# Experts ranked by their rows, in places of 192 down to 32 rows, with four products side by side at 32 rows

## The chip, the core and the metric

The kernel runs on one core of a Trainium2 chip. The metric is the time of one execution on the device, in microseconds, as a median of three runs. TensorE multiplies matrices: the weights of a product (at most 128 rows of contraction by 128 columns) are loaded first, and the other operand of up to 512 columns streams past them into a PSUM bank. VectorE, ScalarE and GpSimd work on elements, and DMA queues bring the weights from HBM; the queue of SyncE issues the loads that matter here.

## The reference

Two transformer blocks on 512 tokens of width 1024 in float32. The first has two feed-forward layers and two attentions, the second a convolution and a chunked recurrence and then a mixture of 32 experts in four groups. Every token chooses a group, and two experts in it; each expert is a gated feed-forward layer of width 512. The change concerns only this last part.

```python
def hierarchical_moe(h, rg_w, rg_b, re_w, re_b, w_gate, w_up, w_down):
    ...
    expert_id = grp[:, None] * EXPERTS_PER_GROUP + top_idx.astype(jnp.int32)
    ...
    counts = jnp.zeros((N_EXPERTS,), jnp.int32).at[e_flat].add(1)
    starts = jnp.cumsum(counts) - counts
    ...
    def expert_block(args):
        xb, e = args
        a = xb @ w_gate[e]
        u = xb @ w_up[e]
        return (jax.nn.silu(a) * u) @ w_down[e]

    ys = lax.map(expert_block, (xs, block_expert)).reshape(n_slots, D)
    ys = ys * slot_gate[:, None].astype(ys.dtype)
    out = jnp.zeros((T, D), ys.dtype).at[slot_tok].add(ys)
...
def second_block(x, ...):
    for l in range(DEPTH):
        h = rmsnorm(x, norm_mix_g[l])
        x = x + hybrid_mixer(h, ...)
        h = rmsnorm(x, norm_ffn_g[l])
        x = x + hierarchical_moe(h, ...)
    return rmsnorm(x, final_norm_g)
```

`top_idx` are the two best experts of the chosen group, so there are 1024 pairs of token and expert. With the reference's inputs they are spread very unevenly: an expert gets between 0 and 150 rows, and five more than 64 beside the first two.

## The kernel before

`route` computes the logits, chooses, and sorts the 1024 pairs by expert: `xs` holds the chosen rows, already transposed, in the order of the experts. Since the counts are known only on the chip, the program is a fixed list of 32 steps (`SLOTS`), each with one place: a number of rows for one expert. Which expert a place gets is worked out in `route`, in a row of small VectorE operations (`wl_...`), and ends in the list `wl` (the expert and the first row of every place), which SyncE reads for the address of a load and ScalarE for the rows.

Steps 0 and 1 take up to 64 rows each of experts 0 and 1, so that their weights can be loaded before the routing is known. Of the other 30 places, five have 128 rows (steps 6, 11, 16, 21, 26) and 25 have 64. An expert with 128 rows or more takes places of 128, the rest goes to places of 64, and what doesn't fit goes through a loop behind the steps; with these inputs the loop does not run.

A place needs six tiles of 1 MB of its expert: `gate` and `up`, two each, and two of `down`. `e_advance` issues a load as soon as a buffer of the three rings (13 tiles in all) is free; a tile is given back by the product that used it last. So there are 192 loads, in the order of the steps.

Step `i` is written out in this order: gate and up of step i+1 (`e_gu`, eight chunks of 128 contraction rows), its activation (`e_act`), down of step i (`e_down`, four chunks), and `keep`. Products are in float32. At 64 rows the bank is split: gate goes to partitions 0 to 63 and up to 64 to 127, which uses two different halves of the array's columns; at 128 rows each product uses all columns and a bank of its own. Between the chunks of gate and up stand, at chunk 0, the transposes of step i's activation (`e_turn`), and behind chunks 3, 5 and 7 three of the four spreads of the place kept in the step before; the fourth stands behind the first chunk of down.

`keep` takes the result of down out of its bank in two parts, a rounded one (ScalarE, `y`) and what is left (VectorE, `y`), and builds `pick`, a matrix that says which row belongs to which token. `spread` multiplies the two, 128 tokens at a time, and VectorE adds the two banks of that to the tokens (`x`). Its products take operands of a rounded format and 128 columns of weights, and their banks come from `po` and `mm` in turn, and `tp`. There are three `mm` banks, two `sc`, two `tp` and one `po`. All products are recorded on line 302, so the tiles' names tell them apart.

## Time and profile before

| | |
|---|---|
| three runs | 2005.28, 2005.52, 2007.22 us |
| median | 2005.52 us |
| the profiled execution | 2004.82 us, its span 2003.0 us |
| busy in the span: TensorE, VectorE, ScalarE | 1894.3 (95%), 1087.9 (54%), 636.4 us (32%) |
| mean granted clock of TensorE | 0.978 |
| loads of experts | 192, of 1024 KB |

The profile is of one execution, and its times are counted from the start of its span. The experts' loads are issued from 1399.9 to 1942.8, and the products with expert weights end near 1976. The page divides the span into 40 slices: in those of the experts the loads move 355 to 420 GB/s, where the rest of the program has mostly 60 to 130.

### The profile page before, as it was taken

How to read it: one execution, taken by the hardware profiler on the slowest of the kernel's cores; microseconds unless marked ns; L12 is line 12 of the kernel's file. 1: busy time of each engine (PE TensorE's matmuls, PEld its weight loads, DVE VectorE, ACT ScalarE, POOL GpSimd, SP SyncE). 2: the span in 40 equal slices, each digit the busy share in tenths (PEclk: the TensorE clock that was granted, in tenths of full speed). 3: DMA queues.
4: the chain of work that ended last, by engine and by line, in shares of the span. 5: the costliest groups of instructions: out<-in, count | busy, mean ns of one | idle time of the engine just before them, and what ended most of it. 6: DMA issues, size and time to landing. Idle time of an engine off the chain costs nothing.

```text
span 2003.0 us, 22137 instructions
## 1 busy us (share of the span) xinstructions
PE 1894.3 (95%) x8372; PEld 1299.0 (65%) x8372; DVE 1087.9 (54%) x1655; ACT 636.4 (32%) x1006; POOL 381.8 (19%) x293
## 2 busy tenths in 40 slices
PE   7999999999999999999999988779799999999995
PEld 5888888887777788888888766657543333333331
DVE  6443344423668565443444599988544444444445
ACT  4322233325555443331223333433232111111112
POOL 2000000106654351000001456643210000000001
PEclk9999999999999999999999998889999999999997
DMA  5234222322222122222222211111799999999991
GB/s 178 85 129 153 92 97 93 126 85 93 81 68 75 64 93 97 101 89 106 86 104 101 97 63 43 42 42 54 288 355 420 419 397 391 380 397 378 384 359 43
DMA packets 52440, 337.85 MB, mean 169 GB/s; under 512 B 5868, under 2 KB 8724, under 8 KB 13804
## 3 DMA queue, kind: packets, MB, share of 16 engines
q1 hardware_dynamic: 48396, 324.04, 42.2%
q0 software_dynamic: 3072, 9.24, 1.5%
q10 hardware_dynamic: 864, 3.15, 0.4%
q8 instruction: 67, 1.10, 0.2%
q14 instruction: 41, 0.34, 0.0%
HBM read 332.18 MB, written 8.16 MB: 170 GB/s over the span
## 4 chain that ended last, share of the span: by engine, by line
PE 81%; DVE 14%; issue 2%; ACT 1%; DMA 1%; POOL 1%; SPq 0%; POOLq 0%; ACTq 0%; DVEq 0%
PE mm L302 65%; PE sc L302 8%; PE tp L302 4%; DVE conv L302 4%; PE po L302 3%; DVE qk L302 2%; DVE score L302 1%; DVE x L302 1%; DVE att_s L302 1%; DVE rs_t L302 1%; DVE rs_y L302 0%; DMA x<-in_xT_dram 0%; DVE hm L302 0%; DMA raw<-in_wd_dram 0%; DVE rs_r L302 0%
## 5 line engine op out<-in xcount | busy, mean ns | idle before, releaser
L302 PE MATMUL mm<-nhi,whi 128*128 128x512 f32 x1120 | 446.8, 399 | 13.3 <-ACT whi L356 9.4
L302 PE MATMUL mm<-nlo,whi 128*128 128x512 f32 x1120 | 439.1, 392 | 1.6 <-DVE nlo L302 1.6
L302 PE MATMUL mm<-nhi,wlo 128*128 128x512 f32 x1120 | 438.5, 392 | 0.7 <-DVE wlo L302 0.7
L356 ACT ACTIVATE whi<-raw 128x1024 fp32r<-128x1024 f32 x220 | 231.2, 1053 | 306.8 <-PE mm L302 119.0
L302 DVE TENSOR_TENSOR wlo<-raw,whi 128x1024 fp32r<-128x1024 f32 x155 | 198.1, 1279 | 208.9 <-ACT whi L356 208.9
L302 PE MATMUL mm<-eraw,xb 128*64 128x512 f32 (+1 forms) x992 | 272.9, 602 | 0.0
L302 PEld LDWEIGHTS mm<-nhi,whi 128*128 128x128 f32 x1120 | 211.8, 189 | 62.7 <-ACT whi L356 9.4
L302 PEld LDWEIGHTS mm<-nlo,whi 128*128 128x128 f32 x1120 | 211.6, 189 | 47.1 <-DVE nlo L302 4.5
L302 PEld LDWEIGHTS mm<-nhi,wlo 128*128 128x128 f32 x1120 | 211.4, 189 | 46.5 <-DVE wlo L302 1.7
L302 POOL TENSOR_TENSOR wlo<-raw,whi 128x1024 fp32r<-128x1024 f32 x65 | 163.5, 2520 | 150.9 <-ACT whi L356 125.1
L302 PEld LDWEIGHTS mm<-eraw,xb 128*64 128x64 f32 (+1 forms) x992 | 81.9, 145 | 130.3 <-issue 120.5
L302 PE MATMUL sc<-eraw,hT 128*64 128x512 f32 (+1 forms) x512 | 140.1, 602 | 0.0
L302 PE MATMUL mm<-hhi,whi 128*128 128x512 f32 x352 | 136.9, 389 | 0.0
L302 PE MATMUL mm<-hlo,whi 128*128 128x512 f32 x352 | 136.9, 389 | 0.0
L302 PE MATMUL mm<-hhi,wlo 128*128 128x512 f32 x352 | 136.9, 389 | 0.0
L302 POOL TENSOR_TENSOR acc<-sq,sq 128x512 f32<-128x512 f32 x6 | 8.7, 1456 | 579.6 <-ACT sq L455 579.6
L302 DVE TENSOR_TENSOR x<-x,po 128x512 f32<-128x512 f32 x62 | 42.6, 687 | 125.4 <-PE po L302 125.3
L302 POOL TENSOR_SCALAR rs_v<-fss 128x1 f32<-128x1 f32 x3 | 0.6, 191 | 515.0 <-ACT eraw L1882 514.8
L1699 ACT ACTIVATE xb<-xs 128x512 f32 (+1 forms) x31 | 21.9, 706 | 233.1 <-PE mm L302 233.0
L302 DVE TENSOR_TENSOR up<-mm,row 128x512 f32<-128x512 f32 x44 | 30.4, 691 | 110.8 <-PE mm L302 110.8
L302 DVE SCALAR_TENSOR_TENSOR conv<-ca,vecs,conv 128x502 f32<-128x502 f32 (+18 forms) x78 | 88.0, 1183 | 0.2
L302 DVE TENSOR_TENSOR y<-sc,y 64x512 fp32r<-64x512 f32 (+1 forms) x64 | 44.1, 689 | 80.7 <-ACT y L1774 62.3
(448 smaller groups left out, 2641.7 us busy)
## 6 DMA issues: line engine op xcount, KB each, us to landing
eraw<-in_we_dram SPq DMA_DIRECT2D x192, 1024.0 KB, 8.0
raw<-in_wd_dram SPq DMA_DIRECT2D x109, 1024.0 KB, 4.8
bias_rows<-bias_by_distance SPq DMA_DIRECT2D x4, 960.0 KB
bias<-bias_rows POOLq DMA_DIRECT2D x12, 256.0 KB, 3.1
x_rows<-x ACTq DMA_DIRECT2D x4, 512.0 KB, 3.5
x<-in_xT_dram SPq DMA_DIRECT2D x3, 512.0 KB, 8.3
raw<-in_wd_dram SPq DMA_DIRECT2D x2, 512.0 KB, 8.9
out_dram<-eraw SPq DMA_DIRECT2D x2, 512.0 KB
```

Source lines behind the costliest of these rows:

```text
L302: return f(*a, **k)
L356: self.nc.scalar.activation(hi, raw, AF.Copy)
L1699: self.nc.scalar.activation(x[:, :, 0:m], self.xs[:, :, ds(row, m)], AF.Copy)
```

## The change

Experts are ranked on the chip by the rows that are left when experts 0 and 1 have had their first 64. The expert of each rank gets a fixed set of places (`RANKS`): 128 and 64 rows for the first, 128 and 32 for the second, 128 for the third, 64 and 32 for the next five, 64 for six, and 32 for the last sixteen. With the two known ahead these are 32 steps again and 39 places: 14 of 64 rows, 22 of 32 and 3 of 128. `EXEC` gives the order of the ranks. All places of a rank stand in one step and use the same six tiles; their chunks follow each other inside the step, chunk by chunk. What is over a rank's capacity goes to the loop behind, which is rewritten for it.

At 32 rows a product has 32 columns of weights and 256 streaming columns, and four of them share a bank: gate left, gate right, up left, up right, each in 32 columns of the array (`gu_chunk`); in down, four quarters (`down_chunk`). `keep` copies and subtracts four quarters of 256 columns, and the spread of such a place uses 64 contraction rows.

The list of places is worked out with two products with triangles and ones (for what goes to the loop) and two that bring expert, first row and last row to the places, where before it was a chain of VectorE operations alone. Three compare tiles stand for two (64, 32 and 128 rows). The rows' tiles `xb` have a ring for each size.

The core of the diff (left out: the constants' new columns, other small operations of the routing, the loop, and lines that only pass the new arguments on):

```diff
-FIRST = 2
-WIDE = 5
-PLACES = 42
-SLOTS = 32
-ITEMS = FIRST + 2 * NE
-WIDE_AT = (6, 11, 16, 21, 26)
+FIRST, FIRST_ROWS = 2, 64
+RANKS = [(128, 64), (128, 32), (128,)] + [(64, 32)] * 5 + [(64,)] * 6 + [(32,)] * 16
+EXEC = (8, 14, 3, 15, 16, 0, 17, 18, 4, 19, 9, 20, 2, 21, 22, 5, 10, 23, 1, 24, 25, 6, 11, 26, 7, 27, 12, 28, 13, 29)
+NL = 32
+
+
+def place_table():
+
+    t = [(-1 - e, 0, FIRST_ROWS, 0) for e in range(FIRST)]
+    for r, ms in enumerate(RANKS):
+        for k, m in enumerate(ms):
+            t.append((r, sum(ms[:k]), m, sum(ms) if k == 0 else 0))
+    t.sort(key=lambda a: {64: 0, 32: 1, 128: 2}[a[2]])
+    of = {}
+    for w, a in enumerate(t):
+        of.setdefault(a[0], []).append((a[1], w, a[2]))
+    of = {r: [(w, m) for _, w, m in sorted(a)] for r, a in of.items()}
+    n = [sum(a[2] == m for a in t) for m in (64, 32, 128)]
+    return t, of, ((0, n[0]), (n[0], n[0] + n[1]), (n[0] + n[1], sum(n)))
+
+
+TABLE, PLACES_OF, GROUPS = place_table()
+P_L = len(TABLE)
+PLACES = P_L + NL
 RINGS = {"raw2": 9, "raw": RAW, "raw3": 2}
...
-        V.tensor_copy(cnt, c[:, 4])
-        F, W, E = FIRST, WIDE, ends
...
+        V.scalar_tensor_tensor(key, left, 32.0, down, op0=ALU.mult, op1=ALU.add)
+        V.scalar_tensor_tensor(cmp[e32, 0:32], key[e32], 1.0, idn, op0=ALU.mult, op1=ALU.mult, accum_out=kcol)
+        V.scalar_tensor_tensor(cmp[e32, 0:32], key[e32], kcol, one, op0=ALU.is_gt, op1=ALU.mult, accum_out=rank)
...
+        pt = self.tp()
+        nc.tensor.matmul(pt[0:32, 0:1], self.tri_b[e32, 0:32], ov[e32, 0:1], start=True, stop=True)
+        nc.tensor.matmul(pt[0:32, 1:2], self.ones_b[e32, 0:32], ov[e32, 0:1], start=True, stop=True)
+        V.tensor_copy(col[e32, 5:7], pt[0:32, 0:2])
...
+        nc.tensor.matmul(pt[0:PLACES, 0:3], M[e32], A[e32], start=True, stop=False)
+        nc.tensor.matmul(pt[0:PLACES, 0:3], ML[e32], B[e32], start=False, stop=True)
...
+            for a in (iota64, iota32, iota[:, 0:128]):
...
-        rest = iter(range(FIRST + WIDE, SLOTS))
-        wide = iter(range(FIRST, FIRST + WIDE))
-        self.ex = [i if i < FIRST else next(wide if i in WIDE_AT else rest) for i in range(SLOTS)]
+        self.steps = [PLACES_OF[-1 - e] for e in range(FIRST)] + [PLACES_OF[r] for r in EXEC]
+        n = len(self.steps)
         o = [(0, j) for j in range(4)]
...
+    def gu_chunk(self, m, ps, x, c, gate, up):
+        s = (c % 4) * 512
+        k = {"start": c == 0, "stop": c == KC - 1}
+        for j, w in enumerate((gate, up)):
+            if m == 32:
+                for f in range(2):
+                    a = 64 * j + 32 * f
+                    self.nc.tensor.matmul(ps[0][a:a + 32, 0:256], x[:, c, 0:32], w[:, s + 256 * f:s + 256 * f + 256], **k)
+            else:
+                o = ps[j] if m == 128 else ps[0][64 * j:64 * j + 64]
+                self.nc.tensor.matmul(o, x[:, c, 0:m], w[:, s:s + 512], **k)
+
+    def down_chunk(self, m, ps, h, c, w):
+        s = (c % 2) * 1024
+        k = {"start": c == 0, "stop": c == 3}
+        if m == 32:
+            o = (c % 2) * 64 + (c // 2) * 32
+            for g in range(4):
+                self.nc.tensor.matmul(ps[0][32 * g:32 * g + 32, 0:256], h[:, o:o + 32],
+                                      w[:, s + 256 * g:s + 256 * g + 256], **k)
+        else:
+            for f in range(2):
+                o = ps[f] if m == 128 else ps[0][64 * f:64 * f + 64]
+                self.nc.tensor.matmul(o, h[:, c * m:(c + 1) * m], w[:, s + 512 * f:s + 512 * f + 512], **k)
...
+        subs = [(m, (self.mm(), self.mm()) if m == 128 else (self.mm(),)) for _, m in self.steps[i]]
         for c in range(KC):
...
+            for (m, ps), x in zip(subs, xs):
+                self.gu_chunk(m, ps, x, c, P[i, j], P[i, j + 1])
...
+        banks = iter((self.sc, self.sc, self.po))
+        subs = [(m, tuple(next(banks)() for _ in range(2 if m == 128 else 1))) for m in ms]
...
+        y = self.yt(F32R)
+        n = 512 if m == 64 else 256
+        for g in range(128 // m):
+            a, o = slice(m * g, m * g + m), slice(m * (g ^ 1), m * (g ^ 1) + m)
+            c = slice(512 * g, 512 * g + 512) if m == 64 else slice(256 * (g % 2), 256 * (g % 2) + 256)
+            nc.scalar.activation(y[a, c], ps[0][a, 0:n], AF.Copy)
+            nc.vector.tensor_sub(y[o, c], ps[0][a, 0:n], y[a, c].bitcast(F32))
         for f in range(2):
-            y = parts[f:f + 1] if len(parts) == 2 else parts
-            r = [y[0][:, 0:512], y[0][:, 512:1024]] if len(parts) == 2 else [y[0][:, 512 * f:512 * f + 512]]
-            for i, a in enumerate(r):
-                self.nc.tensor.matmul(banks[f], w, a, start=first and i == 0, stop=last and i == len(r) - 1)
+            if m == 64:
+                parts.append([(s, y[:, 512 * f:512 * f + 512])])
+            else:
+                a = slice(64 * f, 64 * f + 64)
+                parts.append([(s[a], y[a, 0:512])])
...
+    def spread_to(self, kept, t, banks):
+
+        for f in range(2):
+            r = [a for parts in kept for a in parts[f]]
+            for i, (s, y) in enumerate(r):
+                self.nc.tensor.matmul(banks[f], s[:, t * 128:(t + 1) * 128], y, start=i == 0, stop=i == len(r) - 1)
...
-        banks = self.mm() if t % 2 else self.po(), self.tp()
+    def spread(self, kept, t, mm):
+        banks = self.mm() if mm else self.po(), self.tp()
...
+            both = i + 1 < n and sum(2 if m == 128 else 1 for _, m in self.steps[i + 1]) == 3
+            todo = []
+            if kept:
+                todo = [lambda t=t, k=kept: self.spread(k, t, t == 3 or (t == 1 and not both)) for t in range(4)]
...
+                subs = self.e_gu(i + 1, x, hook)
                 x, xn = xn, rows(i + 3)
-                hn = self.e_act(ps, fac(i + 1))
+                hn = act(i + 1, subs)
...
+            subs = self.e_down(i, hT, lambda c: c % 2 == 0 and todo and todo.pop(0)())
...
+            kept = [self.keep(m, ps, self.tok[:, w:w + 1]) for (w, _), (m, ps) in zip(self.steps[i], subs)]
```

The order of the instructions shows what this does in three places. On TensorE, in a step of 64 rows, before: `mm` from `eraw` is a chunk of gate and up, `sc` one of down, and a product from `y` and `pick` is half a spread.

```order
L302 MATMUL mm_10799<-eraw_10641,xb_10664 64x512
L302 MATMUL mm_10799<-eraw_10651,xb_10664 64x512
L302 MATMUL po_10843<-y_10794,pick_10792 128x512
L302 MATMUL tp_10844<-y_10794,pick_10792 128x512
L302 MATMUL sc_10864<-eraw_10653,hT_10803 64x512 x2
L302 MATMUL mm_10867<-y_10794,pick_10792 128x512
L302 MATMUL tp_10868<-y_10794,pick_10792 128x512
```

After, in a step of 64 and 32 rows, at a spread of a place of 64 rows (`mm_10937` is the place of 64 rows, `mm_10938` that of 32):

```order
L332 MATMUL mm_10937<-eraw_10701,xb_10763 64x512
L332 MATMUL mm_10937<-eraw_10746,xb_10763 64x512
L332 MATMUL mm_10938<-eraw_10701,xb_10774 32x256 x2
L332 MATMUL mm_10938<-eraw_10746,xb_10774 32x256 x2
L332 MATMUL po_10972<-y_10932,pick_10930 128x512
L332 MATMUL tp_10973<-y_10932,pick_10930 128x512
L332 MATMUL mm_10937<-eraw_10791,xb_10763 64x512
L332 MATMUL mm_10937<-eraw_10797,xb_10763 64x512
L332 MATMUL mm_10938<-eraw_10791,xb_10774 32x256 x2
```

Each chunk has its two products at 64 columns and then four at 32, and the spread stands between chunks as before. In the step behind it, a step of 32 rows alone, the spread of a place of 32 rows comes behind four such short chunks:

```order
L332 MATMUL mm_11084<-eraw_10812,xb_10896 32x256 x2
L332 MATMUL mm_11084<-eraw_10845,xb_10896 32x256 x2
L332 MATMUL po_11117<-y_11075,pick_11073 128x512
L332 MATMUL tp_11118<-y_11075,pick_11073 128x512
L332 MATMUL mm_11084<-eraw_10847,xb_10896 32x256 x2
L332 MATMUL mm_11084<-eraw_10877,xb_10896 32x256 x2
```

On ScalarE, `keep` before, at the end of a step of 64 rows (`sc` is the bank of down; what is waited for stands in brackets):

```order
L1774 ACTIVATE y_10694<-sc_10670 64x512 [waits PE_49]
L1774 ACTIVATE y_10694<-sc_10670 64x512 [waits DVE_49]
```

After, at the end of a step of 64 and 32 rows, from the activation of that step (`eg`) to the transposes of the next (`hT`):

```order
L1783 ACTIVATE eg_11029<-mm_10937,fac_10612 64x512
L1783 ACTIVATE eg_11033<-mm_10938,fac_10612 64x256 [waits Activation_49]
L1832 ACTIVATE y_11075<-sc_11037 32x256 [waits PE_49]
L1832 ACTIVATE y_11075<-sc_11037 32x256 [waits DVE_49] x3
L1793 ACTIVATE hT_11090<-tp_11089 128x256 [waits PE_49,Activation_49]
L1793 ACTIVATE hT_11097<-tp_11096 128x128 [waits PE_49,Activation_49]
```

Two copies became four, and each but the first waits for VectorE's subtraction before it. On TensorE in the routing, around the list of places, before:

```order
L302 MATMUL tp_10357<-cmain,wl_col_10344 1x128 x2
L302 MATMUL sc_10360<-cmain,wl_col_10344 128x128 x2
```

After:

```order
L332 MATMUL tp_10339<-wl_ov_10319,tri_b_9778 32x1
L332 LDWEIGHTS ones_b_9779
L332 MATMUL tp_10339<-wl_ov_10319,ones_b_9779 32x1
L332 MATMUL tp_10348<-wl_A_10316,wl_10142 71x3
L332 MATMUL tp_10348<-wl_B_10317,wl_10142 71x3
L332 MATMUL tp_10356<-cmain,wl_out_10351 1x128 x2
L332 MATMUL sc_10359<-cmain,wl_out_10351 128x128 x2
```

Four kinds of products stand ahead of the transposes that were there, with VectorE's copies of their results between them.

## Rows read from the trace of the kernel before

**Rows 1.** Windows: us, busy us (records) by engine, TensorE's clock, DMA share, GB/s.
```profile
1550.00:1600.00 50.00, 50.00 (x188) 19.60 (x188) 22.65 (x36) 8.78 (x15) 0.00 (x0) 1.00 1.01 419
```

**Rows 2.** Waits of the DMA queue from 1400: us in total, times, longest.
```profile
SPq L1673 <- PE mm L302: 280.0, 57, 38.8
```

**Rows 3.** Waits of TensorE from 1450, same columns.
```profile
PEld mm L302 <- DMA eraw<-in_we_dram: 7.2, 15, 0.8
...
PE mm L302 <- DVE y L302: 2.3, 2, 1.5
```

**Rows 4.** Chain of what ended last, from 1380, by line.
```profile
by line: PE mm L302 50.5%; PE sc L302 22.3%; PE tp L302 8.8%; PE po L302 5.3%; DVE x L302 2.6%; issue 1.2%; DVE hm L302 0.9%; POOL rs_t L302 0.8%; DVE scr L302 0.6%; POOL rs_r L302 0.5%; DVE y L302 0.4%; ACT y L1774 0.4%; DVE hmlo L302 0.3%
```

**Rows 5.** Timeline of TensorE, 64-row step: start, us, engine, line, operation, records.
```profile
1598.65 2.79 PE L302 MATMUL mm<-eraw,xb 128*64 128x512 f32 x12
...
1602.04 1.94 PE L302 MATMUL mm<-eraw,xb 128*64 128x512 f32 x8
...
1604.57 1.94 PE L302 MATMUL mm<-eraw,xb 128*64 128x512 f32 x8
...
1607.10 1.08 PE L302 MATMUL sc<-eraw,hT 128*64 128x512 f32 x4
1608.11 0.50 PE L302 MATMUL mm<-y,pick 128*128 128x512 f32 x1
```

**Rows 6.** Timeline of TensorE, 128-row step.
```profile
1551.81 3.59 PE L302 MATMUL mm<-eraw,xb 128*128 128x512 f32 x8
...
1555.47 0.39 PE L302 MATMUL tp<-y,pick 128*128 128x512 f32 x1
1555.69 3.59 PE L302 MATMUL mm<-eraw,xb 128*128 128x512 f32 x8
```

**Rows 7.** Groups by shape from 1350: busy us, mean ns, idle before.
```profile
L302 PE MATMUL mm<-eraw,xb 128*64 128x512 f32 x832 | 200.0, 602 | 0.0
L302 PE MATMUL sc<-eraw,hT 128*64 128x512 f32 x432 | 104.1, 604 | 0.0
...
L302 PE MATMUL mm<-eraw,xb 128*128 128x512 f32 x160 | 72.9, 598 | 0.0
...
L302 PEld LDWEIGHTS mm<-eraw,xb 128*64 128x64 f32 x832 | 52.4, 136 | 96.4 <-issue 91.5 <-DMA eraw<-in_we_dram 3.4
...
L302 PE MATMUL sc<-eraw,hT 128*128 128x512 f32 x80 | 35.9, 592 | 0.0
...
L1737 ACT ACTIVATE hT<-tp 128x256 f32<-128x256 f32 x27 | 10.3, 383 | 7.3 <-PE tp L302 6.9
```

**Rows 8.** Weight load of 36 columns, groups by shape of the whole span.
```profile
L302 PEld LDWEIGHTS po<-x,wr 128*36 128x36 f32 x32 | 1.4, 111 | 3.5 <-issue 2.1 <-DVE x L302 1.4
```

**Rows 9.** Timeline of ScalarE and VectorE in a 64-row step: `keep`, then `e_act`.
```profile
1597.51 0.59 ACT L1774 ACTIVATE y<-sc 64x512 fp32r<-64x512 f32 x1 [4.60 <-PE sc L302]
1598.13 0.68 DVE L302 TENSOR_TENSOR y<-sc,y 64x512 fp32r<-64x512 f32 x1 [2.15 <-ACT y L1774]
...
1598.85 0.59 ACT L1774 ACTIVATE y<-sc 64x512 fp32r<-64x512 f32 x1 [0.75 <-DVE y L302]
...
1599.48 0.69 DVE L302 TENSOR_TENSOR y<-sc,y 64x512 fp32r<-64x512 f32 x1 [0.66 <-ACT y L1774]
...
1607.67 0.68 ACT L1727 ACTIVATE eg<-mm,fac 64x512 f32<-64x512 f32 x1
...
1608.38 0.76 DVE L302 SCALAR_TENSOR_TENSOR eh<-mm,fac,eg 64x512 f32<-64x512 f32 x1
```

**Rows 10.** Timeline of the routing: products, their return, a compare tile.
```profile
1445.40 0.38 PE L302 MATMUL sc<-G,H 128*128 128x16 bf16 x8 [3.76 <-DVE H L302]
1445.82 0.17 DVE L302 COPY rt_part<-sc 128x8 f32<-128x8 f32 x1 [0.48 <-PE sc L302]
...
1465.99 1.22 DVE L302 TENSOR_TENSOR xrow<-iota,rt_q 128x1024 f32<-128x1024 f32 x1
```

**Rows 11.** Timeline of TensorE: the last products with expert weights.
```profile
1972.74 3.65 PE L302 MATMUL sc<-eraw,hT 128*64 128x512 f32 x16
```

More of the change, by code (lines that the diff above doesn't have):

```diff
@@ L1532, in route @@
-        V.tensor_tensor(end, end, bend, ALU.min)
-        V.scalar_tensor_tensor(ex, c3, 0.5, item, op0=ALU.mult, op1=ALU.add)
-        V.tensor_scalar(ex, ex, float(-F), float(NE - 1), op0=ALU.add, op1=ALU.min)
-        more = col[:, 7:8]
-        V.tensor_scalar(more, E[:, ITEMS:ITEMS + 1], float(-SLOTS), 0.0, op0=ALU.add, op1=ALU.max)
+        e32 = slice(0, 32)
+        left, key, cmp = scr[1][:, 0:32], scr[1][:, 32:64], wl[:, 420:500]
+        col = S("wl_col", 16)
+        kcol, rank, cap, rcol, over, cum = (col[e32, j:j + 1] for j in range(6))
@@ L1537, in route @@
+        out3 = S("wl_out", 4)
+        nc.gpsimd.memset(out3, 0.0)
+        ex, row, end = out3[:, 0:1], out3[:, 1:2], out3[:, 2:3]
+        V.tensor_copy(out3[0:PLACES, 0:3], pt[0:PLACES, 0:3])
+        V.tensor_scalar(row, row, w_row, 1024.0, op0=ALU.add, op1=ALU.min)
+        V.scalar_tensor_tensor(end, w_size, row, end, op0=ALU.add, op1=ALU.min)
+        more = col[:, 6:7]
         pt = self.tp()
@@ L1562, in route @@
         self.row1 = self.first_row(1)
-        E8, tm = (self.rpool.tile([128, 8, PLACES], F32, name=self.nm("E8"), tag="E8", bufs=2) for _ in range(2))
+        E8, tm = (self.rpool.tile([128, 8, P_L], F32, name=self.nm("E8"), tag="E8", bufs=2) for _ in range(2))
         Hs = []
@@ L1731, in e_turn @@
[L1731 to L1754 removed]
+        b = slice(0, 128) if m == 128 else slice(64, 128)
@@ L1757, in e_down, with keep @@
                 hook(c)
-        return (ps[0], ps[1]) if m == 128 else (p,)
+        return subs
     def yt(self, dt=F32):
         return self.xpool.tile([128, D], dt, name=self.nm("y"), tag="y", bufs=3)
-    def keep(self, ps, tok):
+    def keep(self, m, ps, tok):
         nc = self.nc
@@ L1855, in moe_blocks @@
+            H = self.yt().rearrange("p (a n) -> p a n", a=8)
+            V.tensor_tensor(H, iota64[:, None, :].to_broadcast([128, 8, 128]), rf[:, :, None].to_broadcast([128, 8, 128]),
+                            ALU.is_equal)
+            p = self.tp()
+            for a in range(8):
+                nc.tensor.matmul(p[:, 0:3], H[:, a], G[:, a], start=(a == 0), stop=(a == 7))
+            V.tensor_scalar(ix, p[:, 0:1], 1024.0, None, op0=ALU.add)
+            V.tensor_copy(fx, p[:, 1:3])
             parts = []
```

307 lines of the change are left out of this document (148 added, 159 removed).

## The prediction

> **What bounds the kernel now.** I read the 50 us windows first. In a window from the middle of the experts [rows 1] TensorE is busy for the whole 50 us, VectorE for 22.65 and ScalarE for 8.78, at a granted clock of 1.00; the DMA engines are full as well, at 419 GB/s. So two things run level there, and the waits tell which one is late. The queue of the expert loads waits 280.0 us for gate and up products to give a tile back [rows 2], while TensorE's weight loads wait 7.2 us in all for expert data, at most 0.8 at a time, and its products 2.3 us for the kept rows [rows 3]: the loads have what slack there is, and TensorE sets the pace. The chain says the same: products with expert weights (`mm`, `sc`) hold 72.8% of it and the spreads' banks (`tp`, `po`) 14.1% [rows 4]. So the change is worth what it does to TensorE's own time and to TensorE's waits; work on VectorE and ScalarE counts where it delays a product.
>
> **What the products save.** An f32 product leaves two records. In a step of 64 rows twelve records take 2.79 us and four 1.08 [rows 5], so eight take 1.71 and four (gate beside up, one chunk) 0.855. A place has 8 such chunks for gate and up and 4 for down: 12 x 0.855 = 10.3 us. For 128 rows eight records and two spread products take 1555.69 - 1551.81 = 3.88 us [rows 6]; less two spread products of 0.23 (one is 1555.69 - 1555.47) that is 3.42, so 1.71 a chunk and 20.5 a place. The counts agree: 832 + 432 and 160 + 80 records [rows 7], and the records at 64 columns cost half of those at 128 (0.24 against 0.45 us). The pair runs fully side by side. Before there are 27 places of 64 rows and 5 of 128: 27 x 10.27 + 5 x 20.53 = 380 us. After there are 14 of 64, 3 of 128 and 22 of 32.
>
> The trace has no product of 32 columns. Its lower bound is four side by side at half the length, 0.428 a chunk, 5.13 a place. The upper bound is that only two run at a time, 0.855, as today. What could hold it back is the weight loads: eight a chunk where four stand now. A load of 64 columns takes 136 ns [rows 7], one of 36 columns 111 ns [rows 8]; the 832 loads keep the loader busy for 52.4 us, not for 832 x 0.136 = 113, so two overlap. Two at a time, eight loads of 0.11 take 0.44 us, about the lower bound, which I therefore take. After: 14 x 10.27 + 3 x 20.53 + 22 x 5.13 = 318 us. **Saved: 62 us.** A place of 32 rows is spread with products on 64 contraction rows and turned with two transposes for four: 4 and 1 us less. In a sentence of its own: the Trainium skill, TensorE: Matmul & The Clock Gate, Part 3 (Measured speedup vs the span model), gives 2.38 times for three column tiles of 32; at the same share four would need, as an estimate, 4 x 0.428 / 3.17 = 0.54 us a chunk, and the time would be about 2050.
>
> **What the order of the products costs.** Between products of equal width nothing is lost [rows 6]: 3.88 - 0.46 = 3.42 is eight records of 0.4275. In a step of 64 rows, eight records and two spread products of 128 columns take 1604.57 - 1602.04 = 2.53 us; products alone are 1.71 + 0.46 = 2.17, so going to 128 columns and back costs 0.36, 0.15 to 0.2 a change [rows 5]. The four records at 1607.10 show how: 1.01 us until the spread product at 1608.11, not 0.855. Now the seven steps with two widths change width twice in each of twelve chunks: five (64, 32) at 24 x 0.147 = 3.5 us, two with a place of 128 at 4.3, together 26 us. When such a place is spread, one bank takes a product on 128 contraction rows and one on 64, so a spread has five changes where it had two: six steps x 4 spreads x 3 x 0.18 = 13 us. **+39 us.** No row shows a change between 64 and 32 columns, whose products use the array in disjoint column groups either way; it may cost nothing, 0.147 is the value at 64 and 128, which I take, and the other end is rival 1. The Trainium skill, TensorEngine Tiling (Array Packing), Tiling Modes, says that "changing tiling mode (not just tile) drains the TensorE"; the 0.36 above agrees, and by this rule rival 1 gets nothing.
>
> **What the kept rows cost.** `keep` copies on ScalarE and subtracts on VectorE in turns: the listing of ScalarE in the part on the change shows each copy but the first waiting for VectorE. At 64 rows this is two rounds of 0.62 + 0.72, 2.7 us (1597.51 to 1600.17) [rows 9]. At 32 rows it is four rounds of half the width: a copy of 256 columns 0.38 (`hT` 128x256 [rows 7]), a subtraction about 0.42 (between half of 0.68 and 0.47), 0.07 between: 3.5 us. The first spread needs all of it, at chunk 3 of the gate and up two steps on: before, 4 x 0.855 and the transposes (0.4), 3.8 us, cover 2.7. Behind a spread TensorE's queue holds everything else, so a shortfall is idle time. Where the next gate and up have 32 rows the cover is 4 x 0.428 + 0.4 = 2.1 us. Over the order of steps: nine times 32 then 32, 3.5 - 2.1 = 1.4, 13 us; three times (64, 32) then 32, 2.7 + 3.5 - 2.1 = 4.1, 12 us; two times (64, 32) then 64, 6.2 - 3.8 = 2.3, 5 us; once each behind (128, 32) and (128, 64), 3.5 and 2.4; the last step but one, 2.5. That is 38 us, against 2.3 today [rows 3]: **+36 us.** VectorE's own work per 32-row step, four spreads of two additions of 512 columns (0.68 each, as `y`), `eh` and the subtractions, is some 8 us of at least 10, so it does not become the bound.
>
> In a step of two places gate and up fill two or three of the three `mm` banks, so the fourth spread, one down chunk later, gets a bank that `e_act` still reads: copy of the rows 0.38, silu 0.68, product `eh` 0.76 [rows 7, 9] and 0.2 between, less the chunk: 1.8 us. Seven times: **+12 us.**
>
> **The rest.** Routing: the chain to the work list gets two more trips from VectorE through TensorE and back (eight small products and the return, 0.42 us [rows 10]) and some more small operations for those removed, and one more compare tile of 1.22 us [rows 10] before the one-hot products: **+2.5 us** (bounds 0 and 5). The last place has 32 rows, and its longer `keep` stands in the open end: **+0.9.** The loads stay 192 of 1 MB. The first 12 are early; 180 x 2.5 us (1.0486 MB at 419 GB/s [rows 1]) from 1464 end near 1914, and today they end near 1950, so at a longer pace they stay hidden.
>
> **Sum:** -62 - 5 + 39 + 36 + 12 + 2.5 + 0.9 = +23.4, less about one for waits that overlap: +22.5. The profiled execution took 2004.82 us with a span of 2003.0; its 2004.82 + 22.5 = 2027, and the median of 2005.52 gives **2028 us**.
>
> **The rivals.**
> 1. *Only a change to 128 columns costs.* The 0.36 is seen there alone. If going between 64 and 32 columns is free, and the mixed spreads lose nothing either (their products follow one another in one bank), 39 us fall away: 2028 - 39 = 1989, faster. It decides from an average of 16 / 240 = 0.07 us a change, where the sum is level (168 changes in chunks, 72 in spreads). For it: the groups of columns are disjoint. Against it: half the new changes involve all rows or all columns, as the measured one does. If only the 64 to 32 changes are free, 14 to 18 us fall away and 2012 is still slower.
> 2. *Four products do not run four abreast.* Loads or the array let two through: 22 x 12 x 0.428 = 113 us more, of which longer cover for `keep` gives back 22 (the 38 us of waits fall to 17): 2028 + 90 = 2117. Against it: the pairs overlap fully, loads included [rows 5, 7]. At half of that loss the time is about 2070.
> 3. *The loads become the bound.* If neither changes nor keeps cost anything, TensorE would need 62 + 5 us less and wait for data: last load near 1916, then the last products and the unchanged end (from 1976.4, behind the last expert products [rows 11], to 2003.0): about 1952.
> 4. *The ranking doesn't fit.* Ranked rows over 192, 160, 128, 96, 64 or 32 go to the loop. The reference's inputs route, ranked and without the first 64 rows of experts 0 and 1, 150, 129, 109, 90, 82, 61, ... 22, 21, 8, ... and fit; the 192 loads of today agree with these counts. One pass would add some 60 us (6 loads of 2.5, 10 of products, and the whole open end of 26.6 again).
> 5. *The waits for `keep` and bank are half of what I count*, the changes cost 0.1: both lie near zero together, -62 - 5 + 24 + 18 + 6 + 3 = -16; half way to that is no change.
>
> **How the numbers follow.** Slower near 2028, anywhere from 2010 to 2070: 0.64. Rival 2, near 2117: 0.06. Rival 1 and 5 on the fast side, near 1989: 0.17. Rival 3: 0.04. Rival 4: 0.01. Within 0.2% (4 us, about what a measurement can tell from no change): 0.08. So faster 0.21, same 0.08, slower 0.71. The range reaches down to rival 1 with a margin, 1984, and up to a chunk of 0.64 us (three quarters of the pairs' price), 2068; rivals 2 and 3 stay out.
>
> **What would show it.** In the trace after: four records of 32 columns start together and a chunk's eight take 0.43 us (0.855: rival 2); in a (64, 32) step a pair of chunks takes 0.855 + 0.428 + 0.29 (1.28: rival 1); TensorE's products wait some 35 to 40 us for `y` and about 12 for `eh`; the loads wait for TensorE still. It would be wrong if those waits were under 20, if changes cost under 0.07, or if more than 192 loads stood there.

## The result, and where the time went

The changed kernel takes 2076.99 us (median of four, 2076.0 to 2083.79) where the kernel before takes 2006.06 in the same comparison: a ratio of 1.036, with a 95% interval from 1.0338 to 1.0383. The forecast was 2028. It is slower, as forecast, but by 71 us instead of 22. The profiled execution took 2076.0 us with a span of 2074.2, 71.2 more than the 2003.0 of before. The page's busy times:

```profile
PE 1940.5 (94%) x9810; PEld 1304.3 (63%) x9810; DVE 1114.4 (54%) x1730; ACT 648.2 (31%) x1085; POOL 383.0 (18%) x292
```

To find the 71 us I compared the starts of the same instructions in both traces. Four stretches divide the span: up to the product `sc<-G,H` of the routing; from there to the first gate and up that reads a place's rows (`mm<-eraw,xb`); from there to the end of the last products with expert weights; and the open end. The marks of before are 1445.40 [rows 10], 1475.34 (its row is shown below) and 1976.4 [rows 11]; those of after are here (start, length, engine, line, operation, count, and in brackets idle time before it and what ended it):

```profile
1470.16 0.38 PE L332 MATMUL sc<-G,H 128*128 128x16 bf16 x8 [3.77 <-DVE H L332]
...
1482.47 0.14 POOL L332 MEMSET wl_out<- 128x4 f32 x1
1482.64 0.16 DVE L332 COPY wl_out<-tp 71x3 f32<-71x3 f32 x1 [6.73 <-POOL wl_out L332]
```

```profile
1512.99 1.98 PE L332 MATMUL mm<-eraw,xb 128*64 128x512 f32 x4
```

```profile
2044.86 2.04 PE L332 MATMUL sc<-eraw,hT 128*32 128x256 f32 x32
```

| stretch | before | after | difference |
|---|---|---|---|
| up to `sc<-G,H` | 1445.4 | 1470.2 | +24.8 |
| to the first `mm<-eraw,xb` | 29.9 | 42.8 | +12.9 |
| expert steps, to the end of the last `sc<-eraw,hT` | 501.1 | 533.9 | +32.8 |
| open end | 26.6 | 27.3 | +0.7 |

A third of the loss lies ahead of all work that the change touches. There the same products simply follow each other more slowly. The two traces of one dense stretch, before and then after, one row of each three:

```profile
349.77 0.39 PE L302 MATMUL mm<-hhi,whi 128*128 128x512 f32 x1
...
350.45 0.39 PE L302 MATMUL mm<-hhi,whi 128*128 128x512 f32 x1
...
351.13 0.39 PE L302 MATMUL mm<-hhi,whi 128*128 128x512 f32 x1
```

```profile
349.69 0.39 PE L332 MATMUL mm<-hhi,whi 128*128 128x512 f32 x1
...
350.39 0.40 PE L332 MATMUL mm<-hhi,whi 128*128 128x512 f32 x1
...
351.09 0.39 PE L332 MATMUL mm<-hhi,whi 128*128 128x512 f32 x1
```

Six products take 1.36 us before and 1.40 after; over the whole dense part it is 227 ns a product against 233.

In the routing, VectorE's copy out of the list's bank waited 6.73 us for GpSimd: the tile `wl_out` is cleared by GpSimd, and in GpSimd's queue that stands behind the eight gathers of rows and the clearing of `xs`.

Most of the rest of that stretch is in the products that bring tokens and factors to the places, 32 of them before and 48 after, since there are three sizes for two. Before and after:

```profile
1471.61 3.81 PE L302 MATMUL tp<-xrow,xrow 128*128 128x126 f32 x32 [0.75 <-DVE xrow L302]
1475.34 1.08 PE L302 MATMUL mm<-eraw,xb 128*64 128x512 f32 x4
```

```profile
1504.18 8.88 PE L332 MATMUL tp<-xrow,xrow 128*128 128x42 f32 x48 [1.81 <-DVE xrow L332]
```

Until the next products they take 3.73 us before and 8.81 after. The first 15 of the 48 follow each other at 112 ns, as the 32 did before; near 1506 the granted clock falls to 0.50 (1.2 GHz), and from there they follow at 213. So 16 products more are 1.8 us, and the lower clock 3.3.

In the expert steps the granted clock, 1.00 throughout before [rows 1], is not. Windows of after (columns as in [rows 1]):

```profile
1500.00:1550.00 50.00, 48.14 (x256) 22.32 (x256) 20.25 (x38) 10.63 (x23) 0.00 (x0) 0.86 0.85 330
1550.00:1600.00 50.00, 46.22 (x362) 15.74 (x358) 24.44 (x43) 10.75 (x24) 0.00 (x0) 0.91 1.01 419
...
1750.00:1800.00 50.00, 49.05 (x355) 17.85 (x355) 27.19 (x48) 12.12 (x27) 0.00 (x0) 1.00 1.01 420
1800.00:1850.00 50.00, 47.86 (x240) 16.65 (x239) 16.86 (x29) 5.41 (x12) 0.00 (x0) 0.83 0.75 301
...
1900.00:1950.00 50.00, 47.77 (x280) 15.56 (x278) 24.63 (x42) 8.70 (x20) 0.00 (x0) 0.82 0.83 337
```

What is missing to 1.00, times the length, is 37 us over the expert steps (summed over windows of 10 us); I call it the clock's loss. What it costs in time is somewhat less, as the experiments show. TensorE's own rows in a step of two widths, and in the steps behind it:

```profile
1563.15 3.23 PE L332 MATMUL mm<-eraw,xb 128*64 128x512 f32 x24
1566.31 0.50 PE L332 MATMUL po<-y,pick 128*128 128x512 f32 x1
...
1570.97 1.50 PE L332 MATMUL mm<-eraw,xb 128*32 128x256 f32 x24
1572.40 0.50 PE L332 MATMUL po<-y,pick 64*128 64x512 f32 x1
1574.23 0.46 PE L332 MATMUL tp<-y,pick 64*128 64x512 f32 x1 [1.33 <-ACT hT L1793]
1574.62 1.07 PE L332 MATMUL mm<-eraw,xb 128*32 128x256 f32 x16
1575.62 0.50 PE L332 MATMUL mm<-y,pick 64*128 64x512 f32 x1
...
1586.36 0.49 PE L332 MATMUL po<-y,pick 128*128 128x512 f32 x1
1588.32 0.50 PE L332 MATMUL po<-y,pick 64*128 64x512 f32 x1 [1.46 <-DVE y L332]
...
1590.06 0.50 PE L332 MATMUL tp<-y,pick 64*128 64x512 f32 x1 [0.82 <-DVE y L332]
1590.48 1.33 PE L332 MATMUL mm<-eraw,xb 128*32 128x256 f32 x16
...
1810.06 0.49 PE L332 MATMUL po<-y,pick 64*128 64x512 f32 x1 [1.33 <-DVE y L332]
1811.79 0.50 PE L332 MATMUL tp<-y,pick 64*128 64x512 f32 x1 [0.81 <-DVE y L332]
```

Four products of 32 columns do run four abreast: 24 records, three chunks, from 1570.97 to 1572.40, are 1.43 us, and 16 records, two chunks, from 1574.62 to 1575.62, are 1.00, each with one change to the spread; so a chunk takes 0.43. Two chunks of a (64, 32) step, 1563.15 to 1566.31, take 3.16. Their products alone would take 2 x (0.855 + 0.428) = 2.57, so four changes cost 0.59, or 0.148 each: three between 64 and 32 columns and one to the spread's 128. TensorE's waits in the expert steps (us in total, times, longest):

```profile
PE tp L332 <- DVE y L332: 8.5, 10, 1.3
PE po L332 <- DVE y L332: 8.0, 6, 2.1
PE tp L332 <- ACT hT L1793: 6.7, 5, 1.4
PE tp L332 <- DVE x L332: 1.7, 4, 0.7
```

Together 25 us, half of the 48 counted, and these rows hold nearly all of the 25.1 us that TensorE stood idle in the expert steps (3.6 before). The wait at 1574.23 is for `hT`: that copy stands behind the alternating copies of `keep` in ScalarE's queue, and the second bank of the spread (`tp`) is free only when it is done.

### The profile page after: what moved, and what is told of

It reads as the page before. It is cut to its first block, busy times and chain, and to the rows that moved or that the text cites. A ratio compares the mean times of both kernels' runs of the same rounds, so it can differ in the third digit from the quotient of the medians.

```text
span 2074.2 us, 25179 instructions
## 1 busy us (share of the span) xinstructions
PE 1940.5 (94%) x9810; PEld 1304.3 (63%) x9810; DVE 1114.4 (54%) x1730; ACT 648.2 (31%) x1085; POOL 383.0 (18%) x292
## 4 chain that ended last, share of the span: by engine, by line
PE 76%; DVE 17%; ACT 3%; issue 2%; POOL 1%; DMA 1%; SPq 0%; ACTq 0%; POOLq 0%; DVEq 0%
PE mm L332 62%; PE sc L332 6%; PE tp L332 4%; DVE conv L332 4%; PE po L332 3%; DVE qk L332 2%; DVE y L332 2%; DVE x L332 2%; ACT y L1832 1%; DVE score L332 1%; DVE att_s L332 1%; DVE rs_t L332 1%; DVE eh L332 0%; DMA x<-in_xT_dram 0%; DVE hm L332 0%
## 5 line engine op out<-in xcount | busy, mean ns | idle before, releaser
L332 PE MATMUL mm<-nhi,whi 128*128 128x512 f32 x1120 | 451.8, 403 | 13.5 <-ACT whi L386 9.5
L332 PE MATMUL mm<-nlo,whi 128*128 128x512 f32 x1120 | 444.9, 397 | 1.3 <-DVE nlo L332 1.2
L332 PE MATMUL mm<-nhi,wlo 128*128 128x512 f32 x1120 | 444.3, 397 | 0.7 <-DVE wlo L332 0.7
L332 PE MATMUL mm<-eraw,xb 128*32 128x256 f32 (+2 forms) x1920 | 255.1, 465 | 0.0
L332 PEld LDWEIGHTS mm<-eraw,xb 128*32 128x32 f32 (+2 forms) x1920 | 78.5, 122 | 135.3 <-issue 111.7
L332 PE MATMUL sc<-eraw,hT 128*32 128x256 f32 (+2 forms) x928 | 129.1, 473 | 0.0
L1832 ACT ACTIVATE y<-sc 32x256 fp32r<-32x256 f32 (+1 forms) x110 | 46.9, 426 | 191.5 <-PE sc L332 137.9
L332 DVE TENSOR_TENSOR y<-sc,y 32x256 fp32r<-32x256 f32 (+2 forms) x116 | 57.4, 495 | 91.9 <-ACT y L1832 76.6
L332 PE MATMUL tp<-y,pick 64*128 64x512 f32 (+1 forms) x164 | 79.1, 506 | 15.3 <-DVE y L332 8.5
```

What stands on the lines that cost most here:

```text
L332: return f(*a, **k)
L1832: nc.scalar.activation(y[a, c], ps[0][a, 0:n], AF.Copy)
```

## The experiments

All times are medians, beside the kernel before at 2006 to 2007 us on the same chip. The last three columns are read from the traces: the distance of dense products, the stretch from `sc<-G,H` to the first `mm<-eraw,xb`, and the expert steps from there to the last `sc<-eraw,hT` record's start, with the clock's loss in them.

| run | us | dense product, ns | routing, us | experts, us (clock's loss) |
|---|---|---|---|---|
| before | 2006 | 227 | 29.9 | 500.5 (0) |
| after | 2077.0 | 233 | 42.8 | 533.5 (37) |
| e1_pad | 2052.6 | 227 | 42.8 | 533.3 (37) |
| e2_before32 | 2029.5 | 233 | 30.2 | 500.5 (0) |
| e8_before64 | 2031.6 | 233 | 30.1 | 500.5 (0) |
| e8_before128 | 2030.2 | 232 | 29.5 | 500.5 (0) |
| e11_right32 | 2047.0 | 227 | 42.8 | 521.2 (23) |
| e12_before_right32 | 2030.6 | 233 | 30.2 | 500.5 (0) |
| e3_early | 2070.5 | 233 | 36.6 | 529.8 (34) |
| e3_early2 | 2049.1 | 227 | 36.7 | 536.1 (40) |
| e4_fill | 2034.7 | 227 | 42.9 | 517.1 (3) |
| e5_masks | 2035.0 | 227 | 42.8 | 524.0 (23) |
| e6_pairs | 2019.8 | 227 | 42.8 | 499.1 (15) |
| e7_all | 2025.8 | 233 | 36.6 | 491.7 (5) |
| e9_late | 1982.3 | 227 | 36.7 | 470.5 (4) |
| e10_late4 | 1981.0 | 227 | 36.6 | 466.8 (4) |

The clock's loss differs between executions of the same steps (23 to 40 us in after, e1_pad, e3_early, e3_early2 and e11_right32, which share them), so a difference of some 10 us in these runs is not put down to an edit unless the loss is taken off first. A us of loss is not a us of time: from e11_right32 to e3_early2 the loss grows by 17.8 us (22.5 to 40.3) and the steps by 14.9, which is 0.84. With this estimate the 37 us of after cost some 31, and the steps that these runs share would take 502 us without them.

**The dense part.** The built programs differ ahead of the routing in one thing: the constants of the routing shrank from 114 to 44 columns, and everything behind them in that pool moved by 288 bytes. The weight tiles `whi` and `wlo` start at 57056 before and at 56768 after, 224 and 192 beyond a multiple of 256 bytes; the streaming operands start at 147424, 225248 and so on, all 224 beyond one, in both.

```diff
-        self.rt_cst = S("rt_const", 44)
+        self.rt_cst = S("rt_const", 52)[:, 0:44]
```

> The changed kernel with 32 unused bytes per partition in the pool of constants, nothing else: the weight tiles of the dense part (whi, wlo) then start at 32 past a multiple of 64 bytes, as in the kernel before, and not at a multiple of 64. Theory A (the start of these tiles sets the pace of the dense products): their distance goes from 233 ns back to 227, the routing starts some 25 us earlier, and the time is about 2052. Theory B (the longer program, or something else upstream): the distance stays at 233 and the time at 2077.

2052.6 us: 32 bytes that nobody uses are worth 24 us. The reverse, in the kernel before:

```diff
-        self.rt_cst = S("rt_const", 114)
+        self.rt_cst = S("rt_const", 124)[:, 0:114]
```

> The kernel before with 32 unused bytes per partition in the pool of constants, nothing else: the weight tiles of the dense part then start at a multiple of 64 bytes, as in the changed kernel. Theory A: 227 ns become 233, and the time rises by 25 us to about 2031. Theory B: it stays at 2006.

2029.5 us, with nothing else changed. Theory A holds in both directions, and the program's length has no part in it. But my rule for the start, 32 past a multiple of 64, fell with e7_all (below), where the tiles stood at 32 beyond a multiple of 256 and the products took 233 ns. Two more places, with 132 and with 148 columns in place of 124:

> The kernel before with 64 unused bytes per partition ahead of the weight tiles of the dense part, nothing else. Fast have been starts at 224 beyond a multiple of 256 (the kernel before, the run with 32 bytes in the changed kernel), which is also where the streaming operands start (147424, 225248); slow have been 192, 0 and 32 beyond it (the last in e7_all, where 32 beyond a multiple of 64 was thought to be enough). Here the start is 32 beyond a multiple of 256. If what counts is the place against 128 or 256 bytes: 233 ns a product and 2029 us. If it is 64: 227 ns and 2007.

> The kernel before with 128 unused bytes per partition at the same place: the weight tiles start at 96 beyond a multiple of 256. If the period is 128 bytes: 227 ns and 2007 us. If it is 256: 233 ns and 2029.

Both slow (233 and 232 ns). Weights at 0, 32, 96 and 192 beyond a multiple of 256 are slow against a stream at 224, and only 224 is fast. Whether that is a place of its own or the place of the stream, two kernels tell that move the stream instead:

```diff
-            with tc.tile_pool(name="u2", bufs=1, side="right") as self.u2:
+            with tc.tile_pool(name="rpad", bufs=1, side="right") as rpad, \
+                    tc.tile_pool(name="u2", bufs=1, side="right") as self.u2:
+                nc.gpsimd.memset(rpad.tile([128, 8], F32, name="right_pad"), 0.0)
```

> The changed kernel with 32 unused bytes per partition at the other end of the memory, which moves the streaming operands of the dense part (nhi, nlo, hhi, hlo) from 224 to 192 beyond a multiple of 256; its weight tiles stand at 192 as they did. If what counts is that weights and streaming operand start at the same place against 256 bytes: 227 ns a product and about 2052 us. If it is the place of the weights alone: 233 ns and 2077.

> The kernel before with the same 32 bytes at the other end: weights at 224 beyond a multiple of 256 as before, streaming operands at 192. If the same place counts: 233 ns and about 2030 us. If it is the place of the weights alone: 227 ns and 2006.

With the stream at 192 too, the changed kernel's products are back at 227 ns; with the stream at 192 and the weights at 224, those of the kernel before go to 233. So it is the one against the other: of the places tried, only equal ones against 256 bytes are fast. (e11_right32 was run twice, 2042.5 and 2051.6; the table's trace is of the first, whose clock lost 15 us less than that of e1_pad.) Why the memory behaves so, no run here shows.

**The wait for GpSimd.**

```diff
+        self.out3 = S("wl_out", 4)
+        nc.gpsimd.memset(self.out3, 0.0)
         self.tri_b, self.ones_b = S("tri_b", 128, dt=BF16), S("ones_b", 128, dt=BF16)
...
-        out3 = S("wl_out", 4)
-        nc.gpsimd.memset(out3, 0.0)
+        out3 = self.out3
```

> As the run with 32 bytes, and the tile wl_out is cleared on GpSimd at the start of the routing's setup instead of behind the eight gathers. Theory: VectorE's copy out of the list's bank no longer waits 6.7 us for GpSimd, and some of the time at the low clock around it goes too: 6 to 10 us less than that run, about 2044. Rival: the gathers themselves set when the first expert's rows are there, and the time moves by less than 2 us.

2070.5 us, 18 above e1_pad. The wait was gone, but the tile's 32 bytes, now ahead of the weights, had moved these by another 32: 233 ns again. Without the unused bytes the tile itself puts the weights at 224:

> The changed kernel with the tile wl_out cleared on GpSimd at the start of the routing's setup; its 32 bytes now stand ahead of the weight tiles, so these start at 32 past a multiple of 64, as in the run with 32 unused bytes (2052.6). In e3_early the same edit had moved them back to a multiple of 64 by its own 32 bytes. Theory: the wait of 6.7 us for GpSimd goes, with some time at the low clock: 2052.6 less 6 to 10, about 2045. Rival: the gathers set the end of the routing anyway: 2052.

2049.1 us. The routing takes 36.7 instead of 42.8, and the copy waits only for its product (total, times, longest):

```profile
DVE wl_out L332 <- PE tp L332: 0.5, 1, 0.5
```

Of the 12.9 us that the routing had lost, this gives back 6.1. In the 6.8 that stay, the two trips of the list over TensorE are 0.2: the list's transposes come 6.6 us behind `sc<-G,H`, and 6.4 before. 5.5 are the 48 products (9.22 until the next product, at 1483.25), most of which run at the lower clock here too, and 1.1 the third compare tile (1.81 of waiting for `xrow` where it was 0.75):

```profile
1474.03 9.29 PE L332 MATMUL tp<-xrow,xrow 128*128 128x42 f32 x48 [1.81 <-DVE xrow L332]
```

**The clock.**

```diff
                 self.nc.tensor.matmul(banks[f], s[:, t * 128:(t + 1) * 128], y, start=i == 0, stop=i == len(r) - 1)
+                if f == 0 and i == 0:
+                    for _ in range(fill):
+                        self.nc.tensor.matmul(banks[1][:, 0:256], self.ident, self.e_iota[:, 0:256], start=True, stop=True)
...
```

> As the run with 32 bytes, and where a spread of 32 rows would leave TensorE idle, three products of 256 columns (five behind a step of two places) with a result that nobody reads stand behind the first product of the spread: TensorE works through the wait, the wait itself stays. Theory C (the clock falls because TensorE stands idle in these waits): the granted clock stays at 1.00 from 1520 on, and the time falls by 25 to 39 us less a few for filler that is too long, to about 2022. Theory D (the clock falls for what the short products of 32 columns ask of the engine): the falls stay and the time is 2052 or a little more.

2034.7 us, 18 less than e1_pad for 52 products more. In after the clock falls to its lower level (0.50, 1.2 GHz) behind the waits of the spread at 1586 to 1590 (windows of 10 us):

```profile
1570.00:1580.00 10.00, 8.50 (x90) 3.51 (x86) 7.48 (x15) 3.77 (x9) 0.00 (x0) 1.00 1.01 420
1580.00:1590.00 10.00, 7.78 (x73) 2.56 (x69) 4.83 (x10) 3.12 (x8) 0.00 (x0) 1.00 1.01 418
1590.00:1600.00 10.00, 9.94 (x49) 3.68 (x49) 3.84 (x7) 0.70 (x2) 0.00 (x0) 0.56 1.01 420
1600.00:1610.00 10.00, 10.00 (x44) 3.51 (x36) 4.14 (x9) 1.50 (x4) 0.00 (x0) 0.59 1.01 417
```

In e4_fill, at the same place of the program (it starts at 1561 there):

```profile
1550.00:1560.00 10.00, 10.00 (x85) 3.03 (x83) 5.43 (x9) 1.08 (x3) 0.00 (x0) 1.00 1.02 419
1560.00:1570.00 10.00, 9.83 (x90) 5.31 (x92) 5.90 (x11) 3.35 (x8) 0.00 (x0) 1.00 1.01 419
1570.00:1580.00 10.00, 10.00 (x64) 3.97 (x57) 5.63 (x11) 2.34 (x7) 0.00 (x0) 1.00 1.01 415
```

TensorE works through, and the clock stays; in all expert steps 37 us of loss become 3, and these 3 are a rest of the low clock of the routing. With the loss taken off at 0.84 the steps take 514 us against 502, so the filler itself costs some 12: it holds TensorE for 24 us, and the idle time fell only from 25.1 to 14.7, since in five places a wait of 1.2 to 1.4 us stands ahead of the filler and other waits got none.

So idle time as a sum is not what the clock answers to. The three long falls of after (17, 17 and 20 us of the 75 at the lower level) come right behind two waits close together, 1.3 to 1.5 us and 0.8 us, in a spread of two places: the rows at 1588 and 1590, at 1810 and 1811, and again at 1931 and 1933. Single waits of 1.3 us and more are followed by short falls or, as at 1574.23, by none, and in e11_right32 the third of these pairs is followed by none either. e4_fill filled the pairs. What it shows is that work put there keeps the clock up, and that the short products of 32 columns alone don't lower it (theory D); whether it does so by ending the idle time or by being wide products, it cannot tell apart. That waits of a us are not needed for a fall, the next run shows.

**The kept rows.**

```diff
+        if m == 32:
+            y, ss = self.yt(F32R), []
+            for j in range(2):
+                s = self.et("pick", F32R)
+                nc.vector.tensor_scalar(s, self.e_iota, tok, self.halves[:, j:j + 1], op0=ALU.is_equal, op1=ALU.mult)
+                ss.append(s)
+            self.split_act(ps[0][:, 0:256], y[:, 0:256], y[:, 256:512])
...
```

> As the run with 32 unused bytes (2052.6), and keep of a place of 32 rows done with one copy and one subtraction of 128 x 256 instead of four and four in turn; two picks, one for the quarters 0 and 2 and one for 1 and 3, each zero on the other quarters, and a spread with four products of 256 columns per bank. Theory: TensorE's waits of some 21 us in the spreads nearly go, the clock stays at 1.00 from 1500 on (32 us at the level of that run), and the products of a spread take as long as before: about 2003. Rival (the falls come from the steps of two widths, not from the waits): the waits go but the falls stay, about 2033.

2035.0 us (2022.7 to 2042.4). The waits nearly went (6.4 us idle for 25), but a spread of such a place has four products a bank for one, and the clock still fell twice, for 20 of its 23 us of loss. Around the first of these falls:

```profile
1779.02 0.50 PE L333 MATMUL po<-y,pick 128*128 128x512 f32 x1
1779.68 0.35 PE L333 MATMUL po<-y,pick 64*128 64x256 f32 x1 [0.16 <-DVE pick L333]
1780.50 0.61 PE L333 MATMUL po<-y,pick 64*128 64x256 f32 x3 [0.47 <-DVE y L333]
1781.04 1.17 PE L333 MATMUL tp<-y,pick 128*128 128x512 f32 x5
1782.14 1.35 PE L333 MATMUL mm<-eraw,xb 128*32 128x256 f32 x16
1783.42 1.95 PE L333 MATMUL mm<-y,pick 128*128 128x512 f32 x5
```

Waits of 0.16 and 0.47, and at 1783 five products of a spread take 1.88 us (to 1785.30) where those at 1781.04 took 1.10: the low clock has come after short waits in a row of changes of width. Each of the two theories of this run fits a part of it; what exactly the chip requires stays open.

**The changes of width.**

```diff
             for (m, ps), x in zip(subs, xs):
-                self.gu_chunk(m, ps, x, c, P[i, j], P[i, j + 1])
+                for d in (range(c - 1, c + 1) if c % 2 else ()) if mixed else (c,):
+                    self.gu_chunk(m, ps, x, d, P[i, j], P[i, j + 1])
```

(and the same in down.)

> As the run with 32 unused bytes (2052.6), and in the steps of two places the chunks follow each other two and two (two of the first place, two of the second), so that the width changes half as often. Theory (a change between 64 and 32 columns costs the 0.15 us that it costs between 64 and 128): five steps save 12 x 0.147 = 1.8 each and two 2.2, together 13 us, 2040. Rival (what a chunk of a mixed step takes over its parts is not the change of width): 2052.

2019.8 us, 33 less. With the loss taken off at 0.84 the experts take 487 us against 502 in e1_pad: 15 us, 2 of them less idle time, where 13 were expected. Two chunks of each place, which took 3.16 us with four changes, take 1540.63 - 1537.76 = 2.87 with two:

```profile
1537.76 2.94 PE L332 MATMUL mm<-eraw,xb 128*64 128x512 f32 x24
1540.63 0.50 PE L332 MATMUL mm<-y,pick 128*128 128x512 f32 x1
```

Two changes less are 0.29 us, 0.145 each. The rest of the 33 us is the clock, which lost 15 instead of 37, though TensorE still stood idle for 22.9 us. The Trainium skill, TensorEngine Tiling (Array Packing), Tiling Modes, says that a change of tiling mode drains the engine; these rows agree and give the price for 64 against 32 columns, 0.145 us.

> The edits of the three other runs of this call together, with the weight tiles at 32 past a multiple of 64. If they add up: 2052.6 - 8 - 50 - 13 = 1982, faster than the kernel before. If the falls of the clock stay: about 2012.

2025.8 us, 44 above the expected sum. The experts take 491.7 us, below the kernel before, as in e6_pairs, but the dense products were at 233 ns, which is 24 of the 44: the two small tiles and the 32 unused bytes together put the weights at 32 beyond a multiple of 256. And the two-pick spreads of e5_masks cost at least as much in products as the waits they removed were worth: without the clock's loss the experts take 488 us here and 487 in e6_pairs.

**Covering the waits instead.** So the last two runs leave the spread as it is and give it more cover:

```diff
-                elif c % 2 and c > 1 and todo:
+                elif c % 2 and c > 3 and todo:
...
             nc.scalar.activation(y[a, c], ps[0][a, 0:n], AF.Copy)
+        for g in range(128 // m):
+            a, o = slice(m * g, m * g + m), slice(m * (g ^ 1), m * (g ^ 1) + m)
+            c = slice(512 * g, 512 * g + 512) if m == 64 else slice(256 * (g % 2), 256 * (g % 2) + 256)
             nc.vector.tensor_sub(y[o, c], ps[0][a, 0:n], y[a, c].bitcast(F32))
```

> The run with chunks two and two (2019.8), and three things more: the spreads start at chunk 5 of gate and up instead of chunk 3 (so they stand at chunks 5 and 7 and behind the first and third chunk of down); keep issues all copies ahead of the subtractions, so ScalarE is free for hT sooner; and wl_out is cleared early (which also keeps the weight tiles at the fast place). Theory C (waits in the spreads make the clock fall): waits of 20 us become some 8 and the falls of 15 us nearly go: 2019.8 - 6 - 12 - 12 = about 1990. Rival (work moved later meets the banks of the next step): no gain beyond the 6 us of routing, 2014.

1982.3 us, 8 below the expectation, a ratio of 0.9879 (0.9863 to 0.9896) to the kernel before. TensorE's idle time in the expert steps is 7.8 us, and no fall of the clock is left between their first and their last few us. No filler stands here, so less idle time and fewer changes do what it did; which of the edits does how much, this run doesn't tell.

> As e9_late, with four chunks of each place in a row in gate and up of a step of two places (down stays two and two). By the price of a change, eight of the twelve changes left in gate and up... four stay: 4 x 0.147 = 0.6 us for each of seven steps, 4 us less than e9_late; the rival is no difference, because with longer runs the spread waits for less or more at its place.

1981.0 us, a ratio of 0.9873 (0.9856 to 0.9889). The experts take 3.7 us less than in e9_late, as the price of a change says; in the whole time the two can't be told apart. This is the fastest version: the shorter products of the change, most of its changes of width removed, and the waits covered. Its waits of TensorE in the expert steps (total, times, longest), and two of its windows:

```profile
PE tp L332 <- DVE x L332: 5.0, 9, 0.7
PE po L332 <- DVE y L332: 2.3, 2, 1.7
```

```profile
1500.00:1550.00 50.00, 49.43 (x390) 18.46 (x386) 29.88 (x51) 11.26 (x23) 0.00 (x0) 1.00 1.00 411
...
1850.00:1900.00 50.00, 49.43 (x407) 19.26 (x395) 29.17 (x51) 13.27 (x31) 0.00 (x0) 1.00 1.01 410
```

The clock is at 1.00, and the DMA engines are full in both. 192 loads less the 12 early ones, at 2.5 us each [rows 1], are 450 us, and the experts take 467: there is little left to win on TensorE while the loads stay.

## Why the prediction was wrong

**What held.** TensorE sets the pace before. The price of a chunk of 32 columns, taken at the lower bound of 0.428 us, was measured at 0.43. The Trainium skill, TensorE: Matmul & The Clock Gate, Part 3 (Measured speedup vs the span model), gives 2.38 times for three column tiles of 32, from which I had estimated 0.54; the trace shows the full four times, and the measurement decides. The price of a change of width held, 0.145 against 0.147, so rival 1 is excluded: e6_pairs took away half the changes and some 13 us with them. Products and changes together were forecast at -28 us (-62 - 5 + 39). Without the waits, and without the clock's loss at 0.84, the experts went from 501.1 - 3.6 = 497.5 to 533.9 - 31.4 - 25.1 = 477.4: -20. This is a remainder, not a sum of rows, and where the 8 us to the forecast lie stays open.

**The step on the keeps and banks was too large.** +36 and +12 were forecast, +22 came (25.1 less 3.6), and those for `y` are 16.5 us, under the 20 that the prediction itself had named as a sign of being wrong. The first product of a spread needs only half of `y`, and goes ahead of the second; I had let it wait for all four rounds. Behind a step of two places the 4.1 us were 1.46 + 0.82 at 1588.32 and 1590.06. The wait for an `mm` bank, 12 us in the sum, has no row among TensorE's waits. What I had not seen is the wait for `hT` behind the keep's copies, 6.7 us.

**The step that took the clock as given was missing.** I read a granted clock of 1.00 in [rows 1] and worked out every term at it, also the waits, which I myself put at 38 us of idle TensorE. e4_fill and e9_late show that these cost a second time: with work in the pairs of waits, or with most of the waits covered, the falls were gone. This is some 31 of the 71 us (37 of loss at 0.84), the largest part.

**The step on the rest looked only at lines that the change touches.** It held nothing for the dense part, and 24.8 us lay there, through the start of tiles that the change doesn't name. A term that moves 5,000 products by 6 ns each can't be seen in the diff, but the allocation could be compared between the two programs. In the routing the trips over TensorE, which I counted, cost 0.2 us; the clearing of one tile of four columns, which I did not, cost 6.1 behind the gathers in GpSimd's queue, and the one-hot products cost 5.1 more, 3.3 of it by the clock again.

So the sum by what the runs show: +24.8 dense part, +6.1 wait for GpSimd, +5.1 products of the routing, +1.7 for the compare tile, the trips and what lies between, -20 products and changes, +22 waits, +31 clock, +0.7 end: 71 us. It closes because the -20 is what the others leave. Without the dense part and the clock it would be +16, near the forecast's +22, but that is luck: the waits were counted 26 too high, products and changes 8 and the routing 10 too low. Rivals 2, 3 and 4 did not occur: four ran abreast, the loads waited for TensorE, and there were 192 of them. What stays open is which pattern of work the clock answers to (e5_masks), and why equal places against 256 bytes make dense products faster.

## What to carry to other kernels

An idle engine costs its wait and then perhaps the clock: where a change puts waits of one or two microseconds on TensorE, price the falls too, or cover the waits, since here the same idea went from 3.6% slower to 1.3% faster by moving the spreads two chunks later, issuing the copies of `keep` ahead of its subtractions, halving the changes of width and clearing a tile earlier, which also put the weight tiles back at the fast place (24 us). When the size of any constant changes, compare the starts of the big tiles in both programs, and compare the traces from the first instruction on, not from the first changed line. An edit that adds an instruction to a queue is paid by what is already queued there, however small the instruction.

## What the runs showed of the hardware

- Back-to-back products of 128 x 512 in the rounded format follow at 227 ns when weights and streaming operand start at the same place against 256 bytes, and at 232 to 233 ns at the other places tried (weights at 0, 32, 96, 192 against a stream at 224; weights at 224 against a stream at 192): 24 us in this kernel.
- Four products of 32 columns by 256 side by side take 0.43 us in f32, a quarter of the 1.71 that two products of 128 columns by 512 take, which do the same for 128 rows.
- A change between products of 64 and 32 columns costs 0.145 us, about as much as one between 64 and 128 (0.15 to 0.2).
- The clock fell to its lower level behind waits of 1.46 and 0.82 us of TensorE close together, and in one run behind 0.16 and 0.47 in a row of changes of width; with filler in these pairs of waits it did not fall, though 14.7 us of other idle time stayed. Behind single waits of 1.3 us the falls were short, or there was none.
- In the expert steps a us of the clock's loss cost 0.84 us of time (estimate from the two ends of five runs with the same steps). Products of 128 contraction rows and 42 columns that followed each other at 112 ns followed at 213 behind a fall.
